# An adaLN decoder trunk on one core: the condition loaded as rows, the small vectors behind the scale weights, one filler step moved, and the last transfers in quarters

## The chip, the cores and the metric

The kernel runs on one core of one Trainium2 chip. The time is the device time of one execution in microseconds (us). A core has five engines that run side by side, each through its own list of instructions in order: TensorE (PE in the profile, with its weight loads as PEld), VectorE (DVE), ScalarE (ACT), GpSimd (POOL) and SyncE (SP). SP, ACT and POOL can issue DMA transfers, each on a queue of its own. Matmuls write to PSUM; tiles are otherwise in SBUF, 128 partitions wide.

## The reference

One layer with S = 512 tokens, D = 1024 channels, an inner width of 2816, batch 1. Cut to what matters here:

```
cs = silu(c)                                  # c: (1, 1024)
mod = cs @ w_ada + b_ada                      # six vectors of 1024
shift1, scale1, gate1, shift2, scale2, gate2 = split(mod, 6)
h = rmsnorm(x, norm1_g) * (1 + scale1) + shift1
qa, ka, va, qd, kd, vd, ga, gd = split(h @ w_in)
out_a = sliding_window_attention(qa, ka, va, sinks)       # 8 heads, window 128
out_d = diff_attention(qd, kd, vd, lam, diff_subln_g)     # 4 heads, two softmaxes each
merged = sigmoid(ga) * (out_a @ w_branch_swa) + sigmoid(gd) * (out_d @ w_branch_diff)
x = x + gate1 * (merged @ w_out)
h2 = rmsnorm(x, norm2_g) * (1 + scale2) + shift2
x = x + gate2 * ((gelu(conv3(h2 @ w_up_a)) * (h2 @ w_up_g)) @ w_down)
out = rmsnorm(x, final_g)                     # fp32, (1, 512, 1024)
```

All data are fp32. The kernel takes each large product as three products of a high and a low part (high by high, low by high, high by low), so one step of the program is three matmuls in a row, and each weight tile needs a cast to its high part on ACT and a subtraction to its low part on DVE.

## The kernel before

**The head.** The channels lie on the partitions. x comes in transposed as four tiles of 512 KB on SP's queue (line 216), then the weights of shift1 and scale1 for the first 128 channels (lines 202 to 206, tiles named `adaw`), then the first tile of w_in (`w`, line 210), and so on for k = 0 to 7. All small vectors (c, b_ada, the norm gains, the convolution's weights and the gain of the differential heads) come as one tensor `columns`, laid out on the host as 128 x 161 and loaded by one transfer on ACT's queue into the tile `cols` (line 141). `keep_warm(n)` (line 236) runs n matmuls of constants on PE. silu(c) is taken from `cols` on ACT and DVE (lines 255 to 258), spread over the partitions by eight transposes on PE (line 262) and copied to `csb` (lines 319 and 321). Four DVE operations make constants out of `cols` (lines 265 to 269; `cb` is one of them).

For the norm, ACT squares x (line 315), DVE adds pairs of squares (line 316) and PE sums over the partitions by matmuls with a tile of ones (line 304, `sums`). `head_mod` (line 296) takes scale1 of the first 128 channels by eight matmuls on PE, `shift_half` (line 325) takes shift1 by two DVE operations. The root follows on ACT and DVE (lines 331 to 334, 166 to 168), PE spreads it by four transposes (line 340), DVE scales x in two halves (`scale_x`, line 348) and makes the two modulation columns `mod` (line 382 for the scale, line 383 for the shift); ACT writes the modulated tile `hThA` (`h_tile`, line 354), in two halves of 256 tokens for k = 0. The products of w_in (lines 365 and 368) start from there.

**The middle.** The differential attention has four heads with four blocks of queries each (s = 0 to 15). PE takes the scores (`sd`, line 679), DVE adds the distances and takes the maximum (line 690), ACT the exponential (line 705), DVE combines the two maps (lines 708 to 710), PE transposes the result (`td`, line 720), ACT casts it (`aTh`, line 426) and DVE takes the low part (`aTl`, line 427); at a head's end `diff_values` (line 727) takes the product with the values (`od`). Between these, `fill(n)` (line 523) lets PE take n steps of the projection to the gates (`pga`) and of the branch products (`pA`), whose results are gathered by ACT (line 806) and DVE (line 823, `ta`), and whose weights are split at line 120 (`wba_l`, `wga_l`). How many steps stand at which place is set by `DIFF_FILL`:

```
        if n == 0 and h:
            fill(DIFF_FILL[3])
            diff_values(h - 1)
```

The rows of the later modulation vectors (`ra`, line 795) are reduced on DVE in between. Around these written places a scheduler orders DVE, ACT and SP.

**The tail.** After the MLP, the last two blocks of 128 rows are normalised in `last_rows`. For the very last block, DVE scales the first 512 channels (`last_final`, line 1736) and sends them on SP's queue, ACT scales the other 512 (`last_scale2`, line 1740) and sends them on ACT's queue, 256 KB each.

## Time and profile before

| | |
|---|---|
| median of 3 runs | 677.48 us (676.98 to 678.10) |
| profiled execution | 677.35 us |
| its span, first to last instruction | 675.3 us |
| time of it outside the span | 2.0 us |
| granted TensorE clock | 0.998 |
| PE, DVE, ACT, POOL busy in the span | 99%, 84%, 59%, 13% |
| data moved by DMA | 121.78 MB, 180 GB/s on average |

Times in the profile are microseconds from the start of the span. In a row of the timeline stand: start, duration, engine, line, operation, result <- operands, shapes, how many instructions the row joins, and in brackets the idle time of the engine just before, with what ended it. A queue's name (SPq, ACTq, POOLq) marks the issue of a transfer, not the transfer. In a row of the groups, the numbers after the bar are total busy time, the mean of one instruction in ns, and the idle time before them. In a row of the DMA issues they are size of one and the median time from issue to landing.

### The profile page before, as it was taken

To read this page: it belongs to the slowest core of one execution; us is meant where nothing else is said; L and a number is where in the kernel's file an instruction comes from. 1 tells how busy PE (TensorE), PEld (TensorE's weight loads), DVE (VectorE), ACT (ScalarE), POOL (GpSimd) and SP (SyncE) were. 2 spreads that over 40 slices of the span, in tenths; PEclk is the share of its full clock that TensorE was granted. 3 is DMA by queue.
4 is the path that set the end of the run, shared out by engine and by line. 5 is a ranking of instruction groups with operands and counts; after the bars stand their busy time and mean duration, and the time that the engine had idled before them with its cause. 6 is when DMAs were issued, how large, how long until landed. Compare 5 with 4: busy or idle time off the path is not lost.

```text
span 675.3 us, 10792 instructions
## 1 busy us (share of the span) xinstructions
PE 665.8 (99%) x4021; PEld 591.9 (88%) x4021; DVE 564.5 (84%) x1005; ACT 400.3 (59%) x702; POOL 84.9 (13%) x110
## 2 busy tenths in 40 slices
PE   8999999999999999999999999999999999999995
PEld 8888888888887888888899999999999998888885
DVE  6997996778777678954799998888888899979997
ACT  6678787466645333233696656566555566656665
POOL 2000000002203200010020211011111003440300
PEclk9999999999999999999999999999999999999999
DMA  8962231345255697577275987887876558996903
GB/s 351 409 239 73 84 105 63 126 156 174 93 172 204 210 322 252 201 234 251 71 125 130 231 201 194 207 209 158 200 187 179 135 187 200 198 203 190 161 0 125
DMA packets 71876, 121.78 MB, mean 180 GB/s; under 512 B 4208, under 2 KB 48016, under 8 KB 71824
## 3 DMA queue, kind: packets, MB, share of 16 engines
q1 hardware_dynamic: 52960, 95.04, 41.2%
q0 software_dynamic: 18576, 25.71, 22.5%
q8 instruction: 31, 0.51, 0.3%
q10 hardware_dynamic: 288, 0.34, 0.2%
q14 instruction: 21, 0.17, 0.1%
HBM read 118.97 MB, written 2.11 MB: 179 GB/s over the span
## 4 chain that ended last, share of the span: by engine, by line
PE 97%; DVE 2%; DMA 1%; issue 0%; ACT 0%; ACTq 0%
PE up L1202 33%; PE dc L1805 15%; PE av L368 3%; PE oc L1258 2%; PE pgd L123 2%; PE oc L1262 2%; PE oc L1259 2%; PE pgd L125 2%; PE pgd L124 2%; PE pga L125 2%; PE pga L123 2%; PE pga L124 2%; PE aqa L365 2%; PE sd L679 2%; PE sw L581 1%; PE pk L123 1%
## 5 line engine op out<-in xcount | busy, mean ns | idle before, releaser
L1202 PE MATMUL up<-t,m_whi 128*128 128x256 f32 x512 | 93.1, 283 | 0.0
L1202 PEld LDWEIGHTS up<-t,m_whi 128*128 128x128 f32 x512 | 79.9, 192 | 0.0
L1202 PE MATMUL up<-t,m_wlo 128*128 128x256 f32 x256 | 72.4, 283 | 0.0
L1202 PE MATMUL up<-bh,p_whi 128*128 128x256 f32 x232 | 65.7, 283 | 0.0
L1202 PE MATMUL up<-bl,p_whi 128*128 128x256 f32 x232 | 65.7, 283 | 0.0
L1202 PE MATMUL up<-bh,p_wlo 128*128 128x256 f32 x232 | 65.7, 283 | 0.0
L1202 PEld LDWEIGHTS up<-t,m_wlo 128*128 128x128 f32 x256 | 49.2, 192 | 0.0
L1104 POOL DMA_DIRECT2D s<-in_w_up_dram x21 | 27.0, 1361 | 158.4 <-DMA s<-in_w_up_dram 125.3
L1202 PEld LDWEIGHTS up<-bh,p_whi 128*128 128x128 f32 x232 | 44.5, 192 | 0.0
L1202 PEld LDWEIGHTS up<-bl,p_whi 128*128 128x128 f32 x232 | 44.5, 192 | 0.0
L1202 PEld LDWEIGHTS up<-bh,p_wlo 128*128 128x128 f32 x232 | 44.5, 192 | 0.0
L1132 ACT CAST m_whi<-s 128x1024 fp32r<-128x1024 f32 x31 | 32.5, 1047 | 15.7 <-DVE s L1126 9.1
L795 DVE CUSTOM_DVE_ANT_0 ra<-ra,csb 128x1024 f32<-128x1024 f32 x32 | 38.7, 1219 | 2.2 <-DMA ra<-in_w_ada_t_dram 2.0
L1136 DVE TENSOR_TENSOR m_wlo<-s,m_whi 128x1024 fp32r<-128x1024 f32 x31 | 37.8, 1218 | 1.3 <-ACT m_whi L1132 1.3
L1202 PE MATMUL up<-t,p_whi 128*128 128x256 f32 x176 | 32.2, 283 | 0.0
L1202 PEld LDWEIGHTS up<-t,p_whi 128*128 128x128 f32 x176 | 27.4, 192 | 0.1
L705 ACT ACTIVATE sd<-sd,dmx 128x128 f32<-128x128 f32 (+3 forms) x32 | 17.7, 555 | 14.3 <-DVE dmx L690 14.1
L1132 ACT CAST p_whi<-wa 128x1024 fp32r<-128x1024 f32 x18 | 18.8, 1043 | 12.6 <-DMA s<-in_w_up_dram 7.2
L1209 ACT ACTIVATE gT<-a,cols 128x512 f32<-128x512 f32 x22 | 17.6, 813 | 13.4 <-DVE a L1244 13.0
L1136 DVE TENSOR_TENSOR p_wlo<-wa,p_whi 128x1024 fp32r<-128x1024 f32 x18 | 22.0, 1222 | 4.0 <-ACT p_whi L1132 3.3
L1202 PE MATMUL up<-t,p_wlo 128*128 128x256 f32 x88 | 24.9, 283 | 0.0
L1126 DVE TENSOR_TENSOR s<-s,wa 128x1024 f32<-128x1024 f32 x20 | 24.4, 1219 | 0.1
(550 smaller groups left out, 2038.1 us busy)
## 6 DMA issues: line engine op xcount, KB each, us to landing
ra<-in_w_ada_t_dram SPq DMA_DIRECT2D x32, 512.0 KB, 4.0
wa<-in_w_up_dram SPq DMA_DIRECT2D x22, 512.0 KB, 4.2
s<-in_w_up_dram SPq DMA_DIRECT2D x21, 512.0 KB, 4.7
s<-in_w_up_dram POOLq DMA_DIRECT2D x21, 512.0 KB, 6.3
adaw<-in_w_ada_t_dram SPq DMA_DIRECT2D x15, 512.0 KB, 10.2
a<-in_w_up_dram SPq DMA_DIRECT2D x11, 512.0 KB, 4.8
b<-in_w_down_dram SPq DMA_DIRECT2D x10, 512.0 KB, 4.0
w<-in_w_first_dram SPq DMA_DIRECT2D x8, 512.0 KB, 10.2
```

What stands on the lines that cost most here:

```text
L123: nc.tensor.matmul(o, lh, rh, start=start, stop=False)
L124: nc.tensor.matmul(o, lh, rl, start=False, stop=False)
L125: nc.tensor.matmul(o, ll, rh, start=False, stop=stop)
L368: nc.tensor.matmul(acc[i], ht[:, t : t + P], wts[k][w][:, S:], start=start, stop=stop)
L705: nc.scalar.activation(pm[m], pm[m], AF.Exp, bias=mx[:, m : m + 1], scale=-1.0, accum_out=(l0, l1)[m])
L795: nc.vector.tensor_tensor_reduce(r, r, csb, 1.0, 0.0, ALU.mult, ALU.add, late_mod[:, idx : idx + 1])
L1104: nc.gpsimd.dma_start(dst, upblock(*blk), accum_op=ALU.add)
L1126: nc.vector.tensor_add(src, src, R[J, "a11" if name == "m6" else "a12"])
L1132: nc.scalar.copy(W[J, name][0], R[J, SRC[name]])
L1136: nc.vector.tensor_sub(lo, R[J, SRC[name]], hi.bitcast(F32))
L1202: nc.tensor.matmul(o[u], w[:, k, cu], b[:, k], start=name in ("p1", "m5", "p2") and k == 0 and x == 0, stop=k == 3 and x == 2, skip_group_ ...
L1805: nc.tensor.matmul((bank2[u] if o is None else o)[:, sl], a[:, q, cu], b[:, q, sl], start=first_mm and x == 0, stop=last_mm and x == 2, sk ...
```

## The change

1. `columns` is gone. c is loaded as eight rows of 128 (tile `crow`, 4 KB, ACT's queue) and transposed on PE into a PSUM bank that is free then; ACT and DVE read it there. The warming matmuls are 6, then the transpose, then 3.
2. The other 153 columns stand behind the 1024 weights of each row of `w_ada_0`, the scale weights (tile `scale0`, 588.5 KB, on SP's queue in the place of the second `adaw` transfer). POOL copies them out into `cols` and makes the constants and `cb`, five operations in place of DVE's four.
3. In the head the first squares are taken in halves too, the second copy to `csb` and the first modulation column for the shift are moved forward on DVE, and the first modulated tile is made in pieces of 128, 128 and 256 tokens.
4. `fill` takes one step more before the values of the third head; as the steps come off one list, later places hold other steps than before.
5. The last block's transfers are quarters: DVE and ACT work in halves of 256 channels, DVE's halves go on SP's queue, ACT's first half goes on POOL's queue and its second on ACT's.

```diff
-    nc.scalar.dma_start(cols[:, :NCOL], columns)
+    crow = cpool.tile([8, P], F32, name="crow")
+    nc.scalar.dma_start(crow, c[0].rearrange("(k p) -> k p", p=P))
...
+    scale0 = pp.tile([P, D + NCOL], F32, name="scale0")
...
-            src = w_ada_t[(1 - j) * D + k * P : (1 - j) * D + (k + 1) * P, :] if k or j else w_ada_0
-            nc.sync.dma_start(adaw[k][:, j], src)
+            if k or j:
+                nc.sync.dma_start(adaw[k][:, j], w_ada_t[(1 - j) * D + k * P : (1 - j) * D + (k + 1) * P, :])
+            else:
+                nc.sync.dma_start(scale0, w_ada_0)
...
-    keep_warm(10)
+    keep_warm(6)
+    ccol = acc[2][:, :8]
+    nc.tensor.transpose(ccol, crow, ident[:8, :8])
+    keep_warm(3)
...
-    nc.vector.tensor_scalar_add(bsc1, bsc1, 1.0)
-    nc.vector.tensor_scalar_mul(n1g, n1g, -0.5)
-    nc.vector.tensor_scalar_mul(sublnc, sublnc, -0.5 * (1.0 - LAM_INIT))
-    cb = cpool.tile([P, 8], F32, name="cb")
-    nc.vector.tensor_mul(cb, bsc1, n1g)
...
-        for hf in range(2) if p == 3 else (None,):
+        for hf in range(2) if p in (0, 3) else (None,):
...
-        if p == 1:
-            nc.vector.tensor_copy(csb[:, :S], acc[0])
+        if p in (1, 2):
+            nc.vector.tensor_copy(csb[:, (p - 1) * S : p * S], acc[p - 1])
     root_table(sqs[3][:, 0:1])
-    nc.vector.tensor_copy(csb[:, S:], acc[1])
...
     shift_half(0)
+    head_mod(0, HEAD_A)
...
-    head_mod(0, 5)
     for t in range(NT):
         nc.tensor.transpose(acc[7][:, t * P : (t + 1) * P], rst[:, t : t + 1].to_broadcast([P, P]), ident)
-    head_mod(5, KT)
+    head_mod(HEAD_A, KT)
+    nc.gpsimd.tensor_copy(cols[:, :NCOL], scale0[:, D:])
+    nc.gpsimd.tensor_scalar_add(bsc1, bsc1, 1.0)
+    nc.gpsimd.tensor_scalar_mul(n1g, n1g, -0.5)
+    nc.gpsimd.tensor_scalar_mul(sublnc, sublnc, -0.5 * (1.0 - LAM_INIT))
+    cb = cpool.tile([P, 8], F32, name="cb")
+    nc.gpsimd.tensor_mul(cb, bsc1, n1g)
...
+    m = mods[0]
+    nc.vector.scalar_tensor_tensor(m[:, 1:2], m[:, 4:5], m[:, 5:6], bsh[:, 0:1], ALU.add, ALU.add)
     scale_x(0, HALVES[0])
-    m = mods[0]
     nc.vector.tensor_scalar(m[:, 0:1], acc[3][:, 0:1], n1g[:, 0:1], cb[:, 0:1], ALU.mult, ALU.add)
-    nc.vector.scalar_tensor_tensor(m[:, 1:2], m[:, 4:5], m[:, 5:6], bsh[:, 0:1], ALU.add, ALU.add)
     scale_x(0, HALVES[1])
-    for sl in HALVES:
+    for sl in (slice(0, P), slice(P, 2 * P), HALVES[1]):
         h_tile(0, 0, sl)
...
-            fill(DIFF_FILL[3])
+            fill(DIFF_FILL[3] + (h == 3))
             diff_values(h - 1)
...
-        last_final(1, rs1)
-        last_scale2(1, rs1, nc.scalar)
+        for sl, q in ((c0, nc.gpsimd), (c1, nc.scalar)):
+            last_final(1, rs1, sl)
+            last_scale2(1, rs1, q, sl)
```

`last_final` and `last_scale2` take the slice `sl` of the 512 channels in the change, for the operation and for the transfer.

**DVE in the head.** DVE's list from the end of the root to the first low part of a weight tile, before (`rst` is the root, `xT<-xT,av` is scale_x in halves, the two `mod` rows without an ISA are the columns for scale and shift):

```order
L168 SCALAR_TENSOR_TENSOR rst<-rt,r_245 128x4
L325 ISA adaw_98,mod_203<-adaw_98,csb 128x512
L325 ISA mod_203 128x1
L348 TENSOR_TENSOR xT<-xT,av_147 128x256
L382 TENSOR_SCALAR mod_203<-av_143,cols,cb 128x1
L383 SCALAR_TENSOR_TENSOR mod_203<-mod_203,cols 128x1
L348 TENSOR_TENSOR xT<-xT,av_147 128x256
L289 TENSOR_TENSOR wlo_269<-w_0_101,whi_268 128x1024
```

and in the change:

```order
L170 SCALAR_TENSOR_TENSOR rst<-rt,r_249 128x4
L327 ISA adaw_100,mod_200<-adaw_100,csb 128x512
L327 ISA mod_200 128x1
L389 SCALAR_TENSOR_TENSOR mod_200<-mod_200,cols 128x1
L356 TENSOR_TENSOR xT<-xT,av_149 128x256
L391 TENSOR_SCALAR mod_200<-av_145,cols,cb 128x1
L356 TENSOR_TENSOR xT<-xT,av_149 128x256
L292 TENSOR_TENSOR wlo_274<-w_0_103,whi_273 128x1024
```

The column for the shift (line 383 before, 389 now) has moved from behind the column for the scale to a place ahead of both scalings.

**DVE ahead of the last head's values.** DVE's list from the third block's low part to the fourth's, before (`wba_l` and `wga_l` are low parts of later weight tiles, `ta` gathers a branch product):

```order
L427 TENSOR_TENSOR aTl_2016<-td_2_2145,aTh_2015 128x3x128
L120 TENSOR_TENSOR wba_l<-wba_2185,wba_h 128x1024
L823 SCALAR_TENSOR_TENSOR ta<-ta,pA_2134 128x512
L120 TENSOR_TENSOR wga_l<-wga_2192,wga_h 128x1024
L427 TENSOR_TENSOR aTl_2016<-td_3_2172,aTh_2015 128x4x128
```

and in the change:

```order
L435 TENSOR_TENSOR aTl_2022<-td_2_2157,aTh_2021 128x3x128
L831 SCALAR_TENSOR_TENSOR ta<-ta,pA_2140 128x512
L121 TENSOR_TENSOR wba_l<-wba_2191,wba_h 128x1024
L435 TENSOR_TENSOR aTl_2022<-td_3_2178,aTh_2021 128x4x128
L121 TENSOR_TENSOR wga_l<-wga_2198,wga_h 128x1024
```

The split of `wga` has moved behind the low part `aTl` of the fourth block.

**DVE half a head earlier.** DVE's list around the third block's maxima (line 690 before, 698 now), before:

```order
L120 TENSOR_TENSOR wga_l<-wga_2179,wga_h 128x1024
L690 ISA sd_2_0_2059,dmx_2_2058<-sd_2_0_2052,ddf 128x384
L690 ISA dmx_2_2058 128x1
L690 ISA sd_2_1_2061,dmx_2_2058<-sd_2_1_2053,ddf 128x384
L690 ISA dmx_2_2058 128x1
L823 SCALAR_TENSOR_TENSOR ta<-ta,pA_2025 128x512
```

and in the change:

```order
L121 TENSOR_TENSOR wga_l<-wga_2185,wga_h 128x1024
L831 SCALAR_TENSOR_TENSOR ta<-ta,pA_2031 128x512
L698 ISA sd_2_0_2069,dmx_2_2068<-sd_2_0_2062,ddf 128x384
L698 ISA dmx_2_2068 128x1
L698 ISA sd_2_1_2071,dmx_2_2068<-sd_2_1_2063,ddf 128x384
L698 ISA dmx_2_2068 128x1
```

`ta` has moved ahead of the maxima. On PE one step of three `pA` matmuls has moved from behind the third head's values to a place ahead of them, and one step fewer stands between the last block's scores and its transposes (six where there were seven).

More of the change, by code (lines that the diff above doesn't have):

```diff
@@ L37 @@
 VA_AT = 5
+HEAD_A = 5
 SWA_FILL = (2, 1, 6, 2, 2, 2, 2, 5, 0)
 DIFF_FILL = (3, 2, 4, 2)
-NCOL = 161
+NCOL = 153
 G1COL = NCOL + 16
@@ L52 @@
     x_t: bass.AP,
-    columns: bass.AP,
+    c: bass.AP,
     w_ada_0: bass.AP,
@@ L140 @@
     cols = cpool.tile([P, NCOL + 32], F32, name="cols")
[L141 to L144 removed]
+    crow = cpool.tile([8, P], F32, name="crow")
+    nc.scalar.dma_start(crow, c[0].rearrange("(k p) -> k p", p=P))
+    bsh, bsc1 = cols[:, 0:8], cols[:, 8:16]
+    blate, n1g, n2g = cols[:, 16:48], cols[:, 48:56], cols[:, 56:64]
+    cv, sublnc = cols[:, 64:152], cols[:, 152:153]
     sink = cpool.tile([P, 8], F32, name="sink")
@@ L296, in head_mod @@
             nc.tensor.matmul(
-                acc[3][:, :NB], adaw[0][:, 0, a * P : (a + 1) * P], cs[:, a : a + 1].to_broadcast([P, NB]),
+                acc[3][:, :NB], scale0[:, a * P : (a + 1) * P], cs[:, a : a + 1].to_broadcast([P, NB]),
                 start=a == 0, stop=a == KT - 1,
@@ L1834 @@
 _INS = [
-    "x", "x_t", "columns", "w_ada_0", "w_ada_t", "w_first", "w_tiles", "swa_sinks", "diff_lambda",
+    "x", "x_t", "c", "w_ada_0", "w_ada_t", "w_first", "w_tiles", "swa_sinks", "diff_lambda",
     "w_branch_swa", "w_branch_diff", "w_out", "w_up", "w_down", "final_g",
@@ L1849 @@
         _np.asarray(inputs[name]).reshape(-1, P).T
-        for name in ("c", "b_ada", "norm1_g", "norm2_g", "conv_w", "conv_b", "diff_subln_g")
+        for name in ("b_ada", "norm1_g", "norm2_g", "conv_w", "conv_b", "diff_subln_g")
     ]
     laid = dict(inputs)
-    laid["columns"] = _np.concatenate(by_column, axis=1)
     laid["w_ada_t"] = _np.asarray(inputs["w_ada"])[0].T
```

19 lines of the change are left out of this document (9 added, 10 removed).

## The prediction

> **What bounds the kernel now.** First the page's chain of waits and its busy times, then the chain piece by piece at the three places that the change touches.
>
> ```profile
> PE 97%; DVE 2%; DMA 1%; issue 0%; ACT 0%; ACTq 0%
> PE 665.8 (99%) x4021; PEld 591.9 (88%) x4021; DVE 564.5 (84%) x1005; ACT 400.3 (59%) x702; POOL 84.9 (13%) x110
> ```
>
> PE carries 97% of the chain, and the change takes no product off it. So it can only win or lose where PE stands: before the first product, at a wait in the middle, and behind the last matmul. All three together are small: PE is idle for 675.3 - 665.8 = 9.5 us of the span. I make the sum against the profiled execution, 677.35 us, of which 675.3 is the span; it lies 0.13 under the median, 677.48.
>
> The head, from the chain (the first two rows), the windows (one) and the timeline:
>
> ```profile
> 0.73 4.24 DMA cols<-in_columns_dram
> 11.26 1.35 PE av L296 x10
> ...
> 7.90:8.90 1.00, 1.00 (x12) 1.00 (x11) 1.00 (x2) 0.78 (x2) 0.00 (x0) 1.00 1.03 414
> ...
> 7.18 0.69 DVE L316 TENSOR_TENSOR sq<-sq 128x512 f32<-128x512 f32 x1 [0.31 <-ACT sq L315]
> 8.65 1.15 ACT L315 ACTIVATE sq<-xT 128x512 f32<-128x512 f32 x2 [0.22 <-DMA xT<-in_x_t_dram]
> 11.23 1.38 PE L296 MATMUL av<-cs,adaw 128*128 128x128 f32 x10
> 12.33 0.16 DVE L168 SCALAR_TENSOR_TENSOR rst<-rt,r 128x4 f32<-128x4 f32 x1
> 12.55 0.65 PE L340 MATMUL av<-ident,rst 128*128 128x128 f32 x4
> 13.91 0.28 DVE L382 TENSOR_SCALAR mod<-av,cols,cb 128x1 f32<-128x1 f32 x1 [0.25 <-PE av L296]
> 14.11 0.21 DVE L383 SCALAR_TENSOR_TENSOR mod<-mod,cols 128x1 f32<-128x1 f32 x1
> 14.35 1.09 ACT L354 ACTIVATE hThA<-xT,mod 128x256 fp32r<-128x256 f32 x2 [0.72 <-DVE mod L383]
> 15.01 0.99 PE L368 MATMUL av<-whi,hThA 128*128 128x512 f32 x3 [0.46 <-ACT hThA L354]
> 15.84 0.40 PE L365 MATMUL aka<-hThA,whi 128*128 128x512 f32 x1
> ```
>
> The chain begins with the transfer of `cols`, but it is not alone there: the window has all DMA engines busy (share 1.03, 414 GB/s), ACT waits for x at 8.65, PE for the scale weights at 11.23, DVE for PE's `head_mod` at 13.91, and ACT for the second `mod` column at 14.35. PE's third product waits for the second half of `hThA`: the row of three ends at 16.00, so the third starts near 15.61.
>
> **The head, part by part.** Without `columns` 80.5 KB leave the front of the queues: at 414 GB/s x lands 0.2 us earlier, and with it squares, sums and root, so `rst` is ready near 12.1. But the scale weights now carry 76.5 KB of it back, and they stand behind x: they land as before, near 11.2. The four `rst` transposes follow the five `head_mod` matmuls at once, which takes away only the gap before them, 0.1, and the first `mod` column moves from 13.91 to some 13.8. The second column (0.21 by its row, 0.24 up to ACT's start) no longer stands between it and ACT: ACT starts near 14.05 in place of 14.35. What the smaller pieces make of this:
>
> ```profile
> L354 ACT ACTIVATE hThA<-xT,mod 128x256 fp32r<-128x256 f32 x4 | 2.2, 594 | 0.8 <-DVE mod L383 0.7
> L354 ACT ACTIVATE hThA<-xT,mod 128x512 fp32r<-128x512 f32 x2 | 1.6, 816 | 0.1
> ```
>
> 256 columns more cost 0.22, so a piece of 128 is an estimated 0.48, and the next starts 0.39 behind it (1.09 less 0.594 is 0.50 for 256, less 0.11). The first product comes at 14.05 + 0.48 + 0.05 = 14.6 in place of 15.01, but the third needs the last piece: 14.05 + 2 x 0.39 + 0.59 + 0.05 = 15.47 in place of 15.61. From there PE is dense, so the head gains 0.15, not the 0.4 of its first product; 0.4 is the upper end, if the last piece comes with the same lead. DVE's next work (the first weight's low part) comes forward too, so k = 1 takes nothing of it back.
>
> The lower end comes from POOL. Its chain (copy, three constants, `cb`) starts when the scale weights land, and the first `mod` column waits for it. The nearest rows:
>
> ```profile
> 2.94 0.40 POOL L245 TENSOR_SCALAR_AFFINE_SELECT dsw<-dsw 128x256 f32<-128x256 f32 x1
> ...
> 179.09 0.20 POOL L755 TENSOR_TENSOR rt<-r 128x4 f32<-128x4 f32 x1
> 179.37 0.74 POOL L756 TENSOR_TENSOR rt<-rt,ms 128x4 f32<-128x4 f32 x1
> 180.21 1.07 POOL L757 TENSOR_SCALAR rt<-rt 128x4 f32<-128x4 f32 x1
> 181.37 0.58 POOL L758 TENSOR_TENSOR cols<-rt,r 128x4 f32<-128x4 f32 x1
> ```
>
> With 0.40 for the copy and 0.20 to 0.30 for each of the four, `cb` is there at 11.2 + 0.4 + 1.2 = 12.8, a whole us before it is asked for. With these four durations as they stand (2.75 with their gaps) it is 14.4, and ACT starts at 14.7: the third product comes 0.5 late. With 1.07 for each it is 15.9, 2.0 late. I take no wait: between 11.2 and 13 DVE has only one long operation, so POOL's rows from an empty head are the nearer. The Trainium skill, "GPSIMD Engine Reference", section 1, Specifications, says that GpSimd shares its SBUF interface with VectorE, with contention when a DVE instruction reads two SBUF operands; the spread from 0.20 to 1.07 for one shape agrees, and by that rule the shift reduction, which reads two, would hold POOL up for its 0.68 us.
>
> The four constants taken off DVE's start gain nothing: DVE waits for squares right behind them (0.31 before 7.18).
>
> **The middle.** PE's only stall here, before the last head's values:
>
> ```profile
> 198.73 0.69 DVE L823 SCALAR_TENSOR_TENSOR ta<-ta,pA 128x512 f32<-128x512 f32 x1
> 199.71 0.16 DVE L708 RECIPROCAL dls<-dls 128x1 f32<-128x1 f32 x1 [0.29 <-ACT sd L705]
> ...
> 205.64 0.75 DVE L710 SCALAR_TENSOR_TENSOR sd<-sd,dls,sd 128x512 f32<-128x512 f32 x1
> 209.65 1.22 DVE L120 TENSOR_TENSOR wga_l<-wga,wga_h 128x1024 fp32r<-128x1024 f32 x1
> 210.79 0.68 DVE L427 TENSOR_TENSOR aTl<-td,aTh 128x512 fp32r<-128x512 f32 x1
> ...
> 204.21 0.39 PE L123 MATMUL pA<-outah,wba_h 128*128 128x512 f32 x1
> 204.44 0.39 PE L124 MATMUL pA<-outal,wba_h 128*128 128x512 f32 x1
> 207.44 0.60 PE L720 MATMUL td<-ident,sd 128*128 128x128 f32 x4
> 210.62 0.40 PE L123 MATMUL od<-aTh,vvh 128*128 128x512 f32 x1
> 211.53 0.50 PE L124 MATMUL od<-aTl,vvh 128*128 128x512 f32 x1 [0.51 <-DVE aTl L427]
> ```
>
> Matmuls of a step are 0.23 apart, so a step is 0.69, and the second `od` could have started at 210.85: the stall is 0.68. Two moves bear on it. `wga_l`, 1.14 from its start to the start of `aTl`, goes behind `aTl`. And the extra step puts the scores of blocks three and four 0.69 later on PE, since the steps behind the scores are one fewer up to the transposes. DVE follows from there, 0.69 later through the maxima, the exponential and the combination; `ta`, now ahead of the maxima, fills time in which DVE would wait for the late scores. So `aTl` starts at 210.79 + 0.69 - 1.14 = 210.34 and ends at 211.02 where it ended at 211.47; PE gains 0.45. The combination of block four then ends at 206.39 + 0.69 = 207.08, still 0.36 ahead of the transposes at 207.44; that cover gone, they wait. The ends are 0 (the scores delay what the split frees) and 0.68 (the stall gone).
>
> The splits that the scheduler moved elsewhere stay behind PE's other steps; I cost them at nothing, and one uncovered would cost up to its 1.22.
>
> **The tail.**
>
> ```profile
> 670.81 0.72 ACT L1740 ACTIVATE x<-chain_outl,rse 128x512 f32<-128x512 f32 x1 [0.68 <-DVE rse L168]
> 670.81 0.75 DVE L1736 SCALAR_TENSOR_TENSOR x<-x,rse,fgbr 128x512 f32<-128x512 f32 x1
> 671.56 0.38 ACTq L1741 DMA_DIRECT2D out_dram<-x  x1
> ...
> out_dram<-x SPq DMA_DIRECT2D x3, 256.0 KB, 2.4
> out_dram<-x ACTq DMA_DIRECT2D x1, 256.0 KB, 2.8
> rb<-rs0d POOLq DMA_DIRECT2D x1, 256.0 KB, 3.8
> rs1d<-rs1p POOLq DMA_DIRECT2D x1, 2.0 KB, 3.1
> ```
>
> ACT's transfer lands last, 671.56 + 2.8 = 674.36; the span ends 0.9 behind. In the change the first quarters are ready near 671.3 (half an operation, 0.48) and the second near 671.7. ACT's second quarter is issued 0.14 later than now; at 414 GB/s its half size saves 0.31, landing at 674.2, or nothing, landing at 674.5. POOL's quarter, by the nearest rows, lands at 671.3 + 3.1 = 674.4 or + 3.8 = 675.1; both rows had other traffic beside them, so I take the short end less the share of that, 2.9, and 674.2. The tail gains 0.1; the ends are -0.75 (POOL's 3.8) and +0.5 (every quarter leaves half an operation earlier and the shares add up). In the Trainium skill, "DMA: Bandwidth & Descriptors", section Anatomy of one DMA, a GpSimd transfer takes 2.0 us plus its bytes at 436 GB/s; by that POOL's quarter would land at 671.3 + 2.3 = 673.6, not last, and the tail would hang on ACT's quarter alone. The rows of 3.1 and 3.8 here are longer than it.
>
> **Sum.** 677.35 - 0.15 - 0.45 - 0.1 = 676.65; I say 676.6.
>
> **Rivals.**
> - All three near their upper ends: 677.35 - 0.4 - 0.68 - 0.5 = 675.8. For it: the three causes don't touch each other. Against it: each needs the follower to come early too.
> - POOL's quarter ends last: 677.35 - 0.15 - 0.45 + 0.75 = 677.5. For it: the rows of 3.1 and 3.8. Against it: they are loads or tiny transfers in a busy stretch.
> - POOL's constants come late, the case that ends slower. The mechanism is the wait of the first `mod` column for `cb`; it decides once the chain takes more than 2.5 us from the landing. At 14.4 it gives 677.35 + 0.5 - 0.55 = 677.3, at 15.9 677.35 + 2.0 - 0.55 = 678.8. For it: the row of 1.07. Against it: one long DVE operation in that stretch.
> - The change doesn't cure the middle: the scores come late, the stall stays, 677.35 - 0.25 = 677.1.
>
> **How the numbers follow.** Forecast 0.45, all upper ends 0.25, POOL's quarter 0.12, POOL's constants 0.10, the stall stays 0.08. What can be told from no change is 0.2%, 1.36 us, so faster begins under 676.12: that is the second case and a small part of the forecast, 0.30. Slower begins at 678.84: the far end of POOL's constants or an uncovered split, 0.12. The rest, 0.58, is the same. The range reaches from the upper ends, 675.5, to the slower cases' middle, 678.2.
>
> **What would show it.** Right: ACT's first piece of `hThA` near 14.05 and the third product near 15.5; POOL's `cb` before 13.5; the wait before the second `od` down to 0.2; the last transfer landing near 674.2 on the old scale. Wrong: the `mod` column with POOL named as its releaser; a wait before the `td` of four; POOL's quarter as the end of the chain; or a stall of PE at a place that now has none.

## The result, and the profile after

| | median, us | lowest to highest | runs |
|---|---|---|---|
| before | 677.42 | 676.35 to 678.31 | 18 |
| the change | 678.86 | 677.91 to 679.59 | 18 |

The ratio is 1.0021 [1.0014, 1.0028]: the change is slower by 1.44 us. 676.6 was forecast and a range of 675.5 to 678.2; both are missed, on the slow side. Run again with other kernels the change took 679.19, a ratio of 1.0028 [1.0018, 1.0039].

The profiled execution of the change took 677.91 us, the lowest of its 18. So a second one is set beside it, of the second series (called after2): 678.96 us, near the median. Cut at four landmarks that both programs have, all three add up to their own times:

| us | before | change | after2 |
|---|---|---|---|
| weight load of the last `sw` product (scores of the window attention, end of the first stage) | 99.04 | 99.19 | 100.18 |
| from there to the weight load of the first `up` product of the MLP | 239.88 | 239.11 | 239.08 |
| from there to the last root, `rse` | 331.70 | 331.71 | 331.68 |
| from there to the last landing of an output | 3.74 | 4.35 | 4.43 |
| from there to the end of the span | 0.96 | 1.29 | 1.33 |
| outside the span | 2.03 | 2.26 | 2.26 |
| the execution | 677.35 | 677.91 | 678.96 |

The middle wins 0.8. The tail loses 0.9 to 1.1, and 0.2 more outside the span. The first stage loses 0.15 in one execution and 1.14 in the other. The page of the change has these busy times and this chain of waits:

```profile
PE 665.2 (98%) x4020; PEld 591.1 (87%) x4020; DVE 564.6 (84%) x1003; ACT 400.6 (59%) x705; POOL 85.9 (13%) x116
PE 88%; issue 7%; DVE 2%; DMA 1%; POOL 1%; SPq 0%; POOLq 0%; ACT 0%; DVEq 0%
```

PE is as busy as before (665.2 for 665.8). POOL and its queue are now in the chain of waits. Its last pieces are these two (start, length, what):

```profile
633.33 37.65 issue
670.98 0.61 POOLq L1882
```

This view alone doesn't show that POOL's quarter ends the program. It goes back from the last issue, which is POOL's, along POOL's own list, and counts the 37.65 us in which POOL had nothing to do as issue. b_tail of experiment 1 ends its chain in the same way (37.66 us of issue, then POOL's queue), and there the end comes from SP. What ends the program is read from other rows in experiment 5.

**The head**, timeline of the change:

```profile
6.88 1.06 ACT L318 ACTIVATE sq<-xT 128x1024 f32<-128x1024 f32 x1 [0.48 <-DMA xT<-in_x_t_dram]
10.92 0.32 POOL L344 COPY cols<-scale 128x153 f32<-128x153 f32 x1 [5.89 <-DMA scale<-in_w_ada_dram]
11.97 0.20 POOL L349 TENSOR_TENSOR cb<-cols 128x8 f32<-128x8 f32 x1
13.54 0.28 DVE L391 TENSOR_SCALAR mod<-av,cols,cb 128x1 f32<-128x1 f32 x1
13.85 1.37 ACT L362 ACTIVATE hThA<-xT,mod 128x128 fp32r<-128x128 f32 x3 [0.53 <-DVE mod L391]
14.39 1.38 PE L376 MATMUL av<-whi,hThA 128*128 128x512 f32 x3 [0.30 <-ACT hThA L362]
15.61 0.40 PE L373 MATMUL aka<-hThA,whi 128*128 128x512 f32 x1
```

and of after2:

```profile
7.87 1.06 ACT L318 ACTIVATE sq<-xT 128x1024 f32<-128x1024 f32 x1 [1.42 <-DMA xT<-in_x_t_dram]
15.39 1.38 PE L376 MATMUL av<-whi,hThA 128*128 128x512 f32 x3 [0.30 <-ACT hThA L362]
16.60 0.40 PE L373 MATMUL aka<-hThA,whi 128*128 128x512 f32 x1
```

The number to compare is the fourth product, `aka`, since the first three now stretch over 1.38 us in place of 0.99: 15.84 before, 15.61 here, 16.60 in after2. All of the second one's delay is there in the first row: the squares of x's third tile wait 1.42 us for the transfer, not 0.48. POOL is done with `cb` at 12.17, 1.4 us ahead of its use.

**The middle** of the change:

```profile
207.58 0.60 PE L728 MATMUL td<-ident,sd 128*128 128x128 f32 x4
209.92 0.68 DVE L435 TENSOR_TENSOR aTl<-td,aTh 128x512 fp32r<-128x512 f32 x1
210.52 1.21 DVE L121 TENSOR_TENSOR wga_l<-wga,wga_h 128x1024 fp32r<-128x1024 f32 x1
210.77 0.39 PE L124 MATMUL od<-aTh,vvh 128*128 128x512 f32 x1
211.00 0.39 PE L125 MATMUL od<-aTl,vvh 128*128 128x512 f32 x1
```

`aTl` stands ahead of `wga_l`, and the second `od` follows the first at 0.23, PE's own pace. **The tail** of the change, timeline and DMA issues:

```profile
670.01 0.16 DVE L170 SCALAR_TENSOR_TENSOR rse<-rt,r 128x1 f32<-128x1 f32 x1
670.20 0.91 ACT L1750 ACTIVATE x<-chain_outl,rse 128x256 f32<-128x256 f32 x2 [0.68 <-DVE rse L170]
671.00 0.58 POOL L1751 DMA_DIRECT2D out_dram<-x  x1 [37.67 <-ACT x L1750]
671.14 0.39 ACTq L1751 DMA_DIRECT2D out_dram<-x  x1
```

```profile
out_dram<-x SPq DMA_DIRECT2D x2, 128.0 KB, 1.8
out_dram<-x POOLq DMA_DIRECT2D x1, 128.0 KB, 3.1
out_dram<-x ACTq DMA_DIRECT2D x1, 128.0 KB, 3.2
```

A quarter of 128 KB on ACT's queue takes 3.2 us, longer than the half of 256 KB did before (2.8); experiment 5 finds 0.63 of it in a single late share.

### The profile page after: what moved, and what is told of

It reads as the page before. It is cut to its first block, busy times and chain, and to the rows that moved or that the text cites. A ratio compares the mean times of both kernels' runs of the same rounds, so it can differ in the third digit from the quotient of the medians.

```text
span 675.6 us, 10797 instructions
## 1 busy us (share of the span) xinstructions
PE 665.2 (98%) x4020; PEld 591.1 (87%) x4020; DVE 564.6 (84%) x1003; ACT 400.6 (59%) x705; POOL 85.9 (13%) x116
## 4 chain that ended last, share of the span: by engine, by line
PE 88%; issue 7%; DVE 2%; DMA 1%; POOL 1%; SPq 0%; POOLq 0%; ACT 0%; DVEq 0%
PE up L1210 33%; PE dc L1816 7%; PE av L376 3%; PE pga L124 2%; PE pga L126 2%; PE pga L125 2%; PE pgd L126 2%; PE pgd L124 2%; PE oc L1270 2%; PE oc L1266 2%; PE oc L1267 2%; PE pgd L125 2%; PE aqa L373 2%; PE sd L687 2%; PE sw L589 1%
```

## The experiments

All times are medians, with the ratio to the kernel before in the same series. Where kernels of different series are compared, it is by what each differs from the kernel before of its own series. The diffs show only the lines that carry the edit. None of these kernels leaves work out; h_dummy and m_q_lanes load, and after_pad_dve and b_odd write, data that nothing reads.

### 1. Which part loses: the tail or what stands ahead of it

tail_old is the change with the old last transfers; tail_sp sends the quarter from POOL's queue on SP's; b_tail and b_mid put the quarters and the extra step alone into the kernel before.

```diff
tail_old
-        for sl, q in ((c0, nc.gpsimd), (c1, nc.scalar)):
-            last_final(1, rs1, sl)
-            last_scale2(1, rs1, q, sl)
+        last_final(1, rs1)
+        last_scale2(1, rs1, nc.scalar)
tail_sp
-        for sl, q in ((c0, nc.gpsimd), (c1, nc.scalar)):
+        for sl, q in ((c0, nc.sync), (c1, nc.scalar)):
b_mid
-            fill(DIFF_FILL[3])
+            fill(DIFF_FILL[3] + (h == 3))
```

> The change with the last rows sent as before: two transfers of 256 KB on SP's and ACT's queues, nothing on POOL's. Theory A (the time is lost behind the last matmul, by the quarters): the head and the middle keep the 0.6 us that the profile of the change shows up to the last root, so 677.4 - 0.6 = 676.8 us, 2.0 under the change. Theory B (the time is lost ahead of the tail, in executions other than the one profiled): it stays near 678.8.

> The change with POOL's quarter sent on SP's queue: four quarters, none on POOL's queue. Theory A1 (POOL's queue is what costs): near tail_old or below it, 676.5 to 676.9 us. Theory A2 (the cost is that of four small transfers with 1 KB rows, whatever the queue): 678 or more. Theory B: 678.8.

> The kernel before with the quartered last transfers alone, one of them on POOL's queue. Theory A: the whole loss and no gain from head and middle, 677.4 + 2.0 = 679.4 us. Theory B: no loss, 677.2 to 677.5.

> The kernel before with the extra step before the third head's values alone. Both theories, by the profile of the change: the 0.7 us wait before the last head's second value product is gone, and 677.4 - 0.5 = 676.9 us. If the gain is given back elsewhere in executions that were not profiled (theory B): 677.4 or more.

| | median | ratio |
|---|---|---|
| tail_old | 677.98 | 1.0013 [1.0004, 1.0022] |
| tail_sp | 678.96 | 1.0026 [1.0017, 1.0034] |
| b_tail | 677.68 | 1.0010 [1.0001, 1.0018] |
| b_mid | 676.88 | 0.9996 [0.9987, 1.0005] |

Both places lose, and neither theory holds alone: tail_old lies between the 676.8 of A and the 678.8 of B, b_tail between 677.5 and 679.4. With the old tail the loss is 0.94 us, where the change has 1.44 and, in the second series, 1.93: the tail's part is 0.5 to 1.0. The quarters alone make the kernel before slower, by 0.64. That SP's queue does no better than POOL's doesn't clear POOL's: experiment 5 shows that each pays for something else. The extra step (-0.16 us between the medians) can't be told from nothing.

### 2. What is wrong in the head

In tail_old x's third tile came late, as in after2. Three ways back: the small vectors on ACT's queue again (h_cols), as a transfer of their own behind the scale weights (h_sep), or something else ahead of x (h_dummy). All three start from tail_old.

```diff
h_cols
+        nc.scalar.dma_start(cols[:, :NCOL], columns)
h_sep
+                nc.sync.dma_start(cols[:, :NCOL], columns)
h_cols and h_sep
-    scale0 = pp.tile([P, D + NCOL], F32, name="scale0")
+    scale0 = pp.tile([P, D], F32, name="scale0")
...
-    nc.gpsimd.tensor_copy(cols[:, :NCOL], scale0[:, D:])
h_dummy
+    pad = pp.tile([P, 161], F32, name="pad")
+        nc.scalar.dma_start(pad, x[0][:P, :161])
```

> tail_old (the change with the old last transfers) with the 153 vectors loaded by a transfer of their own on ACT's queue, right behind c, and the scale weights in rows of 4096 bytes; POOL's copy falls away. Theory H1 (the stream of x is uneven in the change because nothing stands ahead of it: in three profiles of the changed head one or several of the 16 shares of x's third tile landed 0.3 to 1.1 us behind the rest, in none of the three of the old head): x's third tile lands together, the first product at 14.6 to 14.8, and the time is 676.6 to 677.0. Theory H2 (the cost is not in x's stream but elsewhere in the new head): it stays near tail_old, 1 us over the kernel before.

> tail_old with a transfer of 80.5 KB into an unread tile added on ACT's queue right behind c, all else as in the change. H1: the shares of x's third tile land together, though 0.2 us of bytes more stand ahead of x; 0.3 to 0.8 us under tail_old, near the kernel before. H2: 0.2 us over tail_old.

> tail_old with the 153 vectors as a transfer of their own on SP's queue right behind the scale weights, whose rows are 4096 bytes again; nothing ahead of x. H1: x's stream is as uneven as in the change, the time near tail_old. Theory H3 (the rows of 4708 bytes are what costs): 676.6 to 677.0.

> The change itself again, for a second profile and as the reference on this chip. H1: 1.4 us over the kernel before, and in the profile a share of x's third tile behind the rest, as in three of three profiles so far. Theory T1 (in the tail, an 8 KB fetch of instructions on one DMA engine holds back that engine's share of the last quarters, by 0.6 us in the profile of the change and 0.7 in that of tail_sp): the same fetch and the same late share again.

h_cols took 677.10 (0.9998 [0.9988, 1.0007]), h_sep 677.51 (1.0008 [0.9999, 1.0017]), h_dummy 678.05 (1.0011 [1.0002, 1.0019]), and the change again 679.19 (1.0028 [1.0018, 1.0039]). The landings of x's third tile, one time for each of the 16 DMA engines, show where the first stage starts late, and that this is not the whole answer:

```
            most of the 16 shares    last share    first product
before        6.88 to  7.06             7.35         15.01
change        6.35 to  6.58             6.86         14.39
after2        6.36 to  6.77             7.85         15.39
tail_old2     6.35 to  6.70             7.78         15.31
h_tile        6.39 to  6.72             7.95         15.49
h_sep         6.46 to  6.93             7.69         15.22
h_dummy       6.79 to  7.66             7.87         15.40
h_cols        6.68 to  6.95             7.27         14.80
```

The first product comes 7.5 to 7.7 us behind the last share, whatever the other fifteen do. A transfer of the same size ahead of x doesn't bring it in (h_dummy, where half of the shares are late). But h_sep has the late share too, and its median is 0.5 us under h_dummy's. What it has not is a scale tile of 4708 B.

### 3. The place in the queue, and the rows of 4708 bytes

h_swap loads x's tiles in the order 0, 1, 3, 2. h_pad fills the rows of the scale weights with zeros to 5120 B, in memory and in the tile.

```diff
h_swap
-    for p in range(KT // 2):
+    for p in (0, 1, 3, 2):
h_pad
-    scale0 = pp.tile([P, D + NCOL], F32, name="scale0")
+    scale0 = pp.tile([P, D + 256], F32, name="scale0")
```

> tail_old with the fourth tile of x loaded ahead of the third; the work still takes them in the old order, so it needs both. Theory P (place in time: some shares of whatever transfer stands third in SP's queue are held up near 5 us): the shares spread first at the third transfer, which is now x's fourth tile, and both land late; time near tail_old, 0.5 to 1.0 over the kernel before. Theory Q (the place in memory: it is the third tile's reads that are slow): the third transfer lands together, within 0.4 us, and the fourth one spreads.

> tail_old with the rows of the scale weights filled up with zeros from 4708 to 5120 bytes (10 x 512). Theory H3 (rows of 4708 bytes cost, whatever is ahead): back by 0.6 us, 677.2 to 677.4. Theory H1' (the cost is that the 78 KB no longer come ahead of x's second tile, and rows do not matter): as tail_old, 677.9 to 678.2.

> tail_old again, beside h_pad2 on one chip. H3 (the rows of 4708 bytes): 0.7 to 1.2 us over the kernel before and over h_pad2, with a late share of x's third tile in the profile. Chance (the difference between tail_old and h_pad was that of two calls): no more than 0.3 from h_pad2.

> h_pad again (rows of 5120 bytes). H3: within 0.4 of the kernel before or under it, x's third tile landing together within 0.5 us. Chance: as tail_old2.

h_swap took 678.98 (1.0031 [1.0019, 1.0042]): again single shares of the transfer that is third in time landed late, at 7.66 and 7.73, though it was another tile; so it is the place in time, not the data's place in memory. h_pad took 676.82 (0.9998 [0.9990, 1.0006]), and again 677.12 (1.0000 [0.9991, 1.0008]); tail_old, run again beside it, 677.85 (1.0009 [1.0000, 1.0018]). The filling takes back 0.7 to 1.1 us, but not by the late share: that was at 6.89 in the first execution of h_pad and at 7.71 in the second. The start of each PE instruction of a kernel less that of the same one in h_pad2 (us at the top: time in h_pad2) shows where it lies:

```
              23      36      50      62      72      83     200
h_tile      +0.16   +0.16   +0.16   +0.16   +0.12   +0.17   +0.17
tail_old    -0.13   +0.09   +0.29   +0.32   +0.42   +0.32   +0.35
tail_old2    0.00   +0.23   +0.42   +0.45   +0.58   +0.46   +0.48
after2      +0.05   +0.27   +0.47   +0.50   +0.63   +0.50   +0.50
```

PE, which waits for nothing there, falls back bit by bit from 23 us on, by 0.6 up to 61.2, just ahead of the scores of the window attention (+0.61 in tail_old2 there, +0.66 in after2), and has some 0.15 of it back by 83. So it must be slower itself. The groups of products between 23 and 62 us say the same; tail_old2 first (behind the bar: total, mean of one in ns, idle before):

```profile
L376 PE MATMUL av<-wlo,hThA 128*128 128x512 f32 x20 | 6.2, 392 | 0.0
L373 PE MATMUL aqa<-hThA,whi 128*128 128x512 f32 x8 | 2.5, 395 | 0.0
L373 PE MATMUL aka<-hThA,whi 128*128 128x512 f32 x4 | 1.6, 396 | 0.0
```

and h_pad2:

```profile
L376 PE MATMUL av<-wlo,hThA 128*128 128x512 f32 x20 | 6.2, 389 | 0.0
L373 PE MATMUL aqa<-hThA,whi 128*128 128x512 f32 x8 | 2.5, 389 | 0.0
L373 PE MATMUL aka<-hThA,whi 128*128 128x512 f32 x4 | 1.6, 389 | 0.0
```

The same products take 3 to 7 ns more, at a granted clock of 1.00 (windows of the change, in the columns: stretch, its length, PE, PEld, DVE, ACT and POOL with their counts, clock, DMA share, GB/s):

```profile
23.00:62.00 39.00, 39.00 (x175) 31.93 (x174) 33.92 (x54) 27.82 (x46) 0.00 (x0) 1.00 0.66 244
```

175 products by 3 ns are 0.5 us.

### 4. The transfer's rows or the tile's place

The two last runs take this apart. h_tile is tail_old with the tile alone lengthened; its transfer still brings rows of 4708 B. b_odd is the kernel before with a tile of 612 B, the length of the vectors, as the first of the same pool, and no transfer changed.

```diff
h_tile
-    scale0 = pp.tile([P, D + NCOL], F32, name="scale0")
+    scale0 = pp.tile([P, D + 256], F32, name="scale0")
...
-                nc.sync.dma_start(scale0, w_ada_0)
+                nc.sync.dma_start(scale0[:, : D + NCOL], w_ada_0)
b_odd
     pp = pool("p1", stack=p1)
+    odd = pp.tile([P, 153], F32, name="odd")
+    nc.gpsimd.memset(odd[:, :8], 0.0)
```

> The kernel of tail_old, but the tile of the scale's weights is 5120 B long in every partition while its transfer still brings rows of 4708 B: only where the next tiles of the pool lie changes. Theory S (the 612 B more shift the tiles behind it to places from which TensorE streams more slowly): its 128x512 products between 23 and 62 us take 389 ns as before, not 392 to 396, PE loses nothing further there against h_pad2, and the median is 677.0 to 677.3, as h_pad's (676.82, 677.12). Theory H3 (the 4708 B rows cost in the transfers): products of 392 to 396 ns, a further +0.45 to +0.6 us between 23 and 72 us, and a median of 677.8 to 678.0, as tail_old's (677.98, 677.85).

> The kernel before, with a tile of 612 B that nothing reads (8 columns of it written once by POOL at the start) as the first of the same pool; no transfer changes. Theory S: the 128x512 products between 23 and 62 us take 392 to 396 ns in place of 389, PE falls back by 0.4 to 0.6 us in that stage and by nothing in the others, and the median rises by 0.4 to 0.6 us (677.4 to 677.7 where the kernel before has 677.0). Theory H3: 389 ns, and the median of the kernel before within 0.2 us.

h_tile took 677.10 (0.9997 [0.9988, 1.0005]), b_odd 677.49 (1.0001 [0.9992, 1.0010], the kernel before 677.30). h_tile's products:

```profile
L376 PE MATMUL av<-whi,hTlA 128*128 128x512 f32 x20 | 6.2, 389 | 0.0
L376 PE MATMUL av<-wlo,hThA 128*128 128x512 f32 x20 | 6.2, 389 | 0.0
```

those of the kernel before, and of b_odd:

```profile
L368 PE MATMUL av<-whi,hTlA 128*128 128x512 f32 x20 | 6.2, 389 | 0.0
L368 PE MATMUL av<-whi,hThB 128*128 128x512 f32 x8 | 2.8, 389 | 0.0
```

```profile
L370 PE MATMUL av<-whi,hTlA 128*128 128x512 f32 x20 | 6.2, 392 | 0.0
L370 PE MATMUL av<-whi,hThB 128*128 128x512 f32 x8 | 2.8, 393 | 0.0
```

The other executions agree: with the tile of 4708 B (the change twice, tail_old twice, tail_sp, h_dummy, h_swap) the 128x512 products between 23 and 62 us take 392 ns in the mean, with one of 4096 (h_cols, h_sep) or 5120 B, or with none (the kernel before, b_mid, b_tail, m_q, m_q_lanes), 389. So it is the place of the tiles behind the longer one. h_tile has the short rows and even a late share (7.95), and its products take 389 ns and its median is h_pad's; b_odd has neither, and its products take 392. By the trace it loses 0.61 us from 22 to 72 us against the kernel before, as expected; the median rose by 0.19, less than the 0.4 to 0.6 expected and within the noise. Its trace gives part of the loss back at 72 to 83 us (0.16) and at the stall near 211 (0.13), where PE waits for DVE in the kernel before anyway.

### 5. What the quarters lose

Two mechanisms were seen in the traces of the first series: a fetch of 8 KB of DVE's instructions in the midst of the last transfers, and the list of waits by which SP ends the program, one for each pair of slots of the DMA queues (a slot is the semaphore that a transfer counts up when it lands). m_q is b_mid with quarters on SP's and ACT's queues; m_q_lanes adds six small loads in the head, which only moves every later transfer on to other slots. after_pad and after_pad_dve are the change with rows of 5120 B, the latter with 24 more DVE instructions at the start, which moves the fetches to other places of the program.

```diff
m_q
-        last_final(1, rs1)
-        last_scale2(1, rs1, nc.scalar)
+        for sl, q in ((c0, nc.sync), (c1, nc.scalar)):
+            last_final(1, rs1, sl)
+            last_scale2(1, rs1, q, sl)
m_q_lanes
+    for i in range(6):
+        nc.sync.dma_start(more[:, 8 * i : 8 * i + 8], swa_sinks[0].partition_broadcast(P))
after_pad_dve
-    nc.vector.memset(warm, 0.0)
+    for _ in range(25):
+        nc.vector.memset(warm, 0.0)
```

> b_mid (the old head, the extra step) with quartered last transfers, all on SP's and ACT's queues. Theory T2 (behind the last landing SP passes a list of waits, one for each queue slot, 0.06 us each; with quarters the last lander's slot stands early in the list, so 7 or 8 waits are left where 2 were): 0.4 to 0.5 us over b_mid's 676.9, that is 677.3 to 677.4, and the landing itself at the same distance from the last root as with halves (3.7 us). Theory A2 (small rows cost on the wire): the landing itself later by 0.3 or more.

> m_q with six small loads added at the end of the head's loads, 4 KB each and unread, which turns the slots of all later transfers by six of eight. T2: the last landers' slots stand at the list's end, the end of the program follows the landing by 0.95 us in place of 1.3 to 1.4, and the time is 0.3 to 0.4 under m_q. A2: no difference from m_q.

> The whole change with the rows of the scale weights filled up to 5120 bytes. What is left of the loss is then the tail's: T1 and T2 together 1.0 us over h_pad2, so 677.8 to 678.0, and 0.9 under the change. In the profile the 8 KB fetch of instructions near 2.6 us behind the last root and one late share of the quarters, as in the change.

> after_pad with 24 instructions more at DVE's start (writes of one column, while DVE has nothing to do), so that DVE comes to the same place of its code 24 instructions earlier. T1 with DVE's code as the one fetched (the change takes 4 instructions off DVE ahead of the tail and adds one in it): the fetch moves out of the last transfers, no late share, the landing 3.8 us behind the last root in place of 4.4, and 0.5 us under after_pad. If another engine's code is fetched there: no change from after_pad.

m_q took 677.05 (1.0002 [0.9993, 1.0010]), m_q_lanes 676.79 (0.9996 [0.9987, 1.0004]), after_pad 678.59 (1.0021 [1.0012, 1.0030]), after_pad_dve 678.11 (1.0012 [1.0003, 1.0021]). after_pad misses its 677.8 to 678.0: the padding brought 0.3 us against the second series of the change and nothing against the first, not 0.9. In its profiled execution the first stage ends 0.83 earlier than in after2 (99.35 for 100.18), but the middle takes 0.4 more and the late share of an output costs more (below). From the start of the last root, in us, the traces have:

| | last landing | SP's list passed | POOL's DRAIN ends | end of the span | fetch |
|---|---|---|---|---|---|
| before | 3.74 | 3.94 | | 4.70 | |
| m_q | 3.83 | 4.33 | | 5.10 | |
| m_q_lanes | 3.86 | 4.00 | | 4.77 | |
| b_tail | 3.80 | 4.37 | 4.22 | 5.13 | |
| after_pad_dve | 3.89 | 4.37 | 4.64 | 5.42 | at -9.7 |
| change | 4.35 | 4.60 | 4.86 | 5.64 | at 2.59 |
| after2 | 4.43 | 4.72 | 4.99 | 5.76 | at 2.60 |
| after_pad | 4.67 | 5.06 | 5.01 | 5.82 | at 2.28 |
| tail_sp | 4.39 | 4.89 | | 5.66 | at 2.62 |

In each the end is 0.76 to 0.78 behind the later one of two columns, SP's list and POOL's DRAIN (a row at the end of POOL's list); where POOL has no quarter its DRAIN ended 34 us before. In the nine executions with the new head and the old tail, which aren't in the table, it is 0.98 to 0.99 behind SP's list, with DVE's last DRAIN at 0.13 us in place of 0.02. So 0.2 us of their time stands there; why is open. Three things stand between landing and end.

**The list** has a fixed order, and each entry is 0.06 us behind the one before. SP's rows of m_q behind its last landing (674.12), and of m_q_lanes behind its own (674.71), as start, ns and the semaphores waited for (the list is passed 0.06 us behind the row `drain`, at SP's next one):

```
m_q         674.14  28  S[102] S[114]      m_q_lanes   674.73  28  S[110] S[104]
            674.20  28  S[105] S[113]                  674.80   7  drain
            674.26  28  S[106] S[112]
            674.32  28  S[107] S[111]
            674.38  28  S[108] S[101]
            674.44  28  S[109] S[103]
            674.50  28  S[110] S[104]
            674.57   7  drain
```

Where the last transfers have slots that stand early in it, all that follow are still to be passed when they land: 0.50 us in m_q, 0.14 in m_q_lanes. This is why m_q's tail is 0.40 longer than that before; between the medians the six loads gained 0.26, within the noise.

**POOL's own end.** POOL issues its quarter, and its DRAIN ends 0.74 to 0.75 us behind that quarter's landing: in the change 674.13 and 674.87, in after2 675.18 and 675.93, in after_pad_dve 674.35 and 675.10. In these three it ends 0.26 to 0.27 behind SP's list and so sets the end. In b_tail its quarter landed early (673.71), and SP's list was later by 0.15.

**The fetch** takes 406 to 691 ns as one packet, and one share of each output under way lands late, as if it waited on the same DMA engine; the trace doesn't name the engine of a share. In the change, ACT's quarter has shares from 673.21 to 673.73 and one at 674.36, POOL's from 673.57 to 673.90 and one at 674.13. In after_pad all three have one, and the one that counts is SP's (673.64, then 675.04), whose slot stands early in the list. In after_pad_dve the fetch had moved to 660.77; none of its shares stands apart, the span ends 5.42 behind the root in place of 5.82, and the median fell by 0.48, as expected. In b_tail and m_q there is no fetch at this place and no late share. (Every kernel has a further fetch at 0.3 to 1.1, which goes with no late share in these two.)

Ahead of the last root DVE has 1000 operations in the change where it had 1003: four constants less, and one addition of squares more, as it is done in halves. With its semaphore rows it is 1211 for 1219. That this moved the fetch there fits after_pad_dve, where 24 more moved it away, but the extra step too changes DVE's rows (1216 in b_mid), so the four constants alone aren't shown to be the reason.

What a late share costs depends on who waits: in the change 0.23 (POOL's quarter, 674.13 for 673.90), in tail_sp 0.70 (SP's last, 675.47 for 674.77). So tail_sp trades POOL's DRAIN for a dearer fetch and the list, and is no faster.

For the change the terms add up: 0.15 by which undisturbed quarters land later (3.89 for 3.74), 0.55 for POOL's DRAIN in place of the short list (0.75 for 0.20), 0.23 for the fetch: 0.93 of 0.94. The quarters themselves brought nothing in any kernel. POOL's quarter in b_tail:

```profile
out_dram<-x POOLq DMA_DIRECT2D x1, 128.0 KB, 2.5
out_dram<-x ACTq DMA_DIRECT2D x1, 128.0 KB, 1.9
```

In the Trainium skill, "DMA: Bandwidth & Descriptors", section Anatomy of one DMA, a GpSimd transfer takes 2.0 us plus its bytes at 436 GB/s; the estimate for POOL's quarter is 2.3, under both the 2.5 here and the 3.1 of the change.

## Why the prediction was wrong, point by point

**The tail** was forecast at -0.1 with ends of -0.5 and +0.75; from the root to the span's end it is +0.94 in the change, +1.06 in after2, and 0.23 more lies outside the span. That part shows in the four executions with both the new head and POOL's quarter (2.22 to 2.26) and in no other (1.76 to 2.04, b_tail with POOL's quarter at 1.91); its cause stays open.

The step that failed is the end of the sum, "the span ends 0.9 behind" the last landing: it was taken as fixed, and it depends on whose transfer lands last. Behind a quarter of POOL's own 1.52 us follow. A term was left out too: POOL's issue starts 0.99 behind the root (671.00), 0.29 behind the end of the operation it waits for (670.71), where the sum has it leave at once, 0.68 behind. The transfer itself was priced near: POOL's quarter took 2.5 in b_tail, 2.9 in after_pad_dve and 3.1 here, where 2.9 was taken; the late share makes the 0.23 between the last two, and why b_tail's was faster isn't shown. On the old scale the last landing is at 674.97 (670.62 + 4.35), where 674.2 was named as the sign. The rival that had POOL's quarter end last named the right place, with 0.75 as its price, and the wrong reason, the transfer's length.

**The scale weights' longer tile** had no term at all: their transfer was priced, the 612 B that the tile grows were not. They cost 0.45 to 0.6 us on the trace (products of 392 to 396 ns in place of 389). Between medians it is 0.7 to 1.1 by tail_old's two against h_pad's two and h_tile's, and 0 to 0.3 by the change against after_pad; part of what lies between is the middle, which differs from execution to execution (by 0.4 between tail_old2 and h_pad2 on the trace); the rest isn't explained.

**The head** was right where its transfers came evenly: in the profiled execution of the change, `aka` came 0.23 earlier (forecast 0.15 for the third product, which stands at 15.27), POOL's constants at 12.17 (forecast 12.8), and ACT's first piece at 13.85 (14.05). The step that failed is "at 414 GB/s x lands 0.2 us earlier". Most shares did, by some 0.5 us (6.35 to 6.58 for 6.88 to 7.06). But the squares wait for the slowest of sixteen. It landed at 7.18 to 7.49 in the six profiled executions with the old head; of the thirteen with the new one (without h_cols, which loads the vectors ahead again) it landed at 7.66 to 7.95 in nine, at 7.37 and 7.50 in two, and earlier than before in two alone, 6.86 and 6.89. That the profiled execution of the change was one of these two is luck. With the late share `aka` came 0.76 later in after2. Why shares of the third transfer stall with the new head is open. It isn't the missing 80.5 KB alone (h_dummy), the vectors' place (h_sep), the rows' length (h_pad2) or the tile (h_swap). h_tile and h_pad, with the rest of the new head and middle and the tiles back in place, are level with the kernel before, with 0.2 us lost at their end (experiment 5): what the head wins in one execution it loses in another.

**The middle** went as forecast, and more, in the two executions of the change: the stall of 0.68 is gone and the stretch from `sw` to `up` is 0.77 and 0.80 shorter (forecast 0.45). What was off is the price by one execution. The kernel before doesn't stall by 0.68 in each: in b_tail, with the same code there, the second `od` follows the first at 0.50, a stall of 0.27, and the stretch is 239.46 in place of 239.88.

```profile
210.63 0.40 PE L123 MATMUL od<-aTh,vvh 128*128 128x512 f32 x1
211.13 0.50 PE L124 MATMUL od<-aTl,vvh 128*128 128x512 f32 x1
```

Of the seventeen executions with the extra step, ten have a stall under 0.1 at this place and seven still one of 0.2 to 0.4. Two of the seven also wait ahead of the `td` of four, the case that was named and left at 0.36 of cover; their stretches are the longest of all, 240.2 (m_q_lanes) and 240.4 (h_cols). h_cols, timeline:

```profile
208.32 0.63 PE L731 MATMUL td<-ident,sd 128*128 128x128 f32 x4 [0.37 <-DVE sd L721]
...
212.17 0.50 PE L126 MATMUL od<-aTl,vvh 128*128 128x512 f32 x1 [0.22 <-DVE aTl L438]
```

Alone (b_mid) the step measured -0.16 us between the medians of the first series, not distinguishable from nothing.

**POOL late**, the rival at the slow end, did not occur: in the change its five operations took 1.25 us from copy to `cb`. The hold by the shift reduction that the prediction describes does exist, and is too short to matter. In h_pad the reduction starts first, and `cb` takes its time, 0.67 in place of 0.20:

```profile
12.09 0.68 DVE L327 CUSTOM_DVE_ANT_0 adaw<-adaw,csb 128x512 f32<-128x512 f32 x1
12.16 0.67 POOL L349 TENSOR_TENSOR cb<-cols 128x8 f32<-128x8 f32 x1
```

So it is in h_pad2, h_tile, after_pad and after_pad_dve (0.67 to 0.74). In the change the two start together (11.96 and 11.97), `cb` takes 0.20, and the reduction 0.75 in place of 0.68. In h_pad `cb` is still 0.86 us ahead of its use at 13.69. A slip in the prediction's sum for this rival changes nothing: the four rows from 179.09 take 2.86 us with their gaps, not 2.75.

By the medians the account is: tail +0.5 to 1.0 (the change less tail_old) or +1.5 (after_pad less h_pad2, in one series), tile 0 to +1.1, head and middle together -0.2 to +0.1 (h_pad, h_pad2 and h_tile against the kernel before), where +1.44 and, in the second series, +1.93 were measured. That tail and tile both lose is shown; how they share the loss is known to half a us. No kernel tried beats the one before: the best, m_q_lanes at 0.9996 [0.9987, 1.0004] and b_mid at the same ratio, can't be told from it.

## What to carry to other kernels

In this kernel a stage that waits for a whole transfer waits for the slowest of its sixteen shares, so read the landings of the shares before a mean rate is turned into a gain, and look at more than one execution before a stall is priced. Where a tile grows, keep its length in a partition at which the products behind it keep their pace, here by 412 B of filling in the tile alone. At a program's end count what isn't in the code: the waits for queue slots and POOL's DRAIN behind the landings, and the instruction fetches that fall among the last transfers.

## What the runs showed of the hardware that was not expected

- **Where a tile lies changes TensorE's pace.** With the tiles of one pool moved on by 612 B, 128x512 products took 392 to 396 ns in place of 389 at the same clock; moved on by 1024 B, 389. Which step counts isn't known (4096 and 5120 B are multiples of 64; 4708 and 612 of 4 only; h_dummy, with 4708 and 644 B, 5352 together, a multiple of 8, has 392 too), and whether PE reads slower by itself or only beside other accesses, wasn't tried. The Trainium skill, "SBUF — State Buffer", section Operand start alignment, asks for a multiple of the element size, and section SBUF: two separate sides says that PE never waits on anyone; neither has a price for it. No wait shows here either (idle 0.0 in the rows), and the products are slower all the same.
- **An instruction fetch can hold back a transfer.** With a fetch of 8 KB (406 to 691 ns) among the last transfers, a share of an output came 0.6 us late in the change and 1.4 in after_pad; with the fetch moved away (after_pad_dve) none did.
- **The end of a program depends on the queue that lands last.** SP passes the slots' semaphores in a fixed order, 0.06 us each (m_q, m_q_lanes), and POOL's DRAIN ends 0.75 us behind the landing of a transfer that POOL issued; the span ends 0.76 to 0.78 behind the later of the two in the executions of the table, 0.98 to 0.99 in the nine with the new head and the old tail.
- **Shares of one transfer are uneven.** Single shares of the third transfer landed up to 1.3 us behind most others; packets of 4 KB took 778 ns in after2 (near 5.6 us) and 978 in tail_old (near 5.0), where the mean is 160 to 170.
